# A hybrid attention layer on one core: c's parts through a view, the first weights ahead of x, one bias addition for tile 0

## The chip, the core and the metric

The kernel runs on one core of a Trainium2 chip. A core has five engines, each with its own instruction queue: TensorE (PE in the profile; PEld is its loading of stationary weights), VectorE (DVE), ScalarE (ACT), GpSimd (POOL) and SyncE (SP, which here only issues transfers). Sixteen DMA engines move data between device memory (HBM) and the on-chip buffer (SBUF). TensorE writes its results to a third memory, PSUM. The engines run side by side and wait for each other through semaphores.

The metric is the device time of one execution in microseconds (us), taken as the median of a few runs.

## What is computed

One decoder layer for 512 positions of width 1024. All its inputs are float32. The part that matters here is the start: the conditioning vector c (1024 numbers) is multiplied by a large matrix, and the first two of the six resulting vectors shift and scale x before the input projection.

```python
mod = c @ w_ada + b_ada
sh1, sc1, gt1, sh2, sc2, gt2 = [m[:, None, :] for m in jnp.split(mod, N_MOD, axis=-1)]

u = x * (1.0 + sc1) + sh1
proj = u @ w_in
...
y_fox = _merge_heads(_forgetting_attention(...))
y_sb = _merge_heads(_stick_breaking_attention(...))
merged = jax.nn.sigmoid(g_a) * (y_fox @ w_fox_proj) + jax.nn.sigmoid(g_b) * (y_sb @ w_sb_proj)
attn_out = merged @ w_o
x = _layer_norm(DEEPNORM_ALPHA * x + (1.0 + gt1) * attn_out, ln1_g, ln1_b)
u2 = x * (1.0 + sc2) + sh2
h = _causal_depthwise_conv(u2 @ w_up, conv_w, conv_b)
h_gate, h_val = jnp.split(h, 2, axis=-1)
ffn_out = (jax.nn.silu(h_gate) * h_val) @ w_down
x = _layer_norm(DEEPNORM_ALPHA * x + (1.0 + gt2) * ffn_out, ln2_g, ln2_b)
```

## The kernel before

**Precision.** [...] So that a product keeps the precision of float32, each operand is split into a high part h (rounded by ScalarE, a copy into the type fp32r) and a low part l (the remainder, one subtraction on VectorE, helper `lo_of`, line 94). A product is then three matmuls: high by high, low by high and high by low. In the names below `wh`, `wl` are the parts of a weight and `uh`, `ul` those of u.

**Tiling.** The width of 1024 is cut into KT = 8 tiles of 128 rows. The opening works through them one after the other, j = 0 to 7. For each tile it loads two pieces of the modulation matrix (`wa`, one for the shift and one for the scale), the rows of x (`xt`, 128x512) and the first weights of the input projection (`raw`, 128x904: 904 columns, the last 8 being those of the forget gate). VectorE multiplies `wa` by c and sums along the row (`mod_sum`, line 231), which gives one shift and one scale per row (`modc`). From x it makes u and its two parts, and TensorE adds the tile's products to eight accumulators in PSUM (`grp`, line 349, 23 matmuls for a tile). Attention, the output projection and the gated MLP follow; they are not touched.

**How c reaches all partitions.** `mod_sum` needs the whole of c in every one of the 128 partitions. c arrives as 8 rows of 128 (`c8s`, line 102). VectorE splits it into three parts of type bf16 whose sum is c to full precision. They stand in rows 0 to 7, 32 to 39 and 64 to 71 of a tile `chl`: the first is a rounded copy (line 122, written as an addition of zeros), then comes the remainder in float32 (`c1`, line 123), the same remainder as bf16 (line 124), and what is left after that (line 125). Eight small matmuls (line 225) with a matrix `sel` of ones in rows k, 32+k and 64+k add the three parts and spread row k over all partitions, four into each of the two accumulators `grp[6]` and `grp[7]`. For tile 0 `mod_sum` reads c straight from these accumulators; later tiles read a copy of it in SBUF (`cbc`, line 325, made by ScalarE). For tile 0 the sums are taken in halves of 512 columns, so there are four: e is the half and q the vector (0 the shift, 1 the scale). After them two operations (line 277) add for each vector its two halves and the bias column `bcols`. ScalarE has added 1 to the columns of the scales beforehand (line 127).

**Warming matmuls.** TensorE runs matmuls without use (`heat`, line 220, on a tile of zeros): `WARM[0]` = 7 at the start, `WARM[1]` = 3 after the eight that spread c, and `WARM[2]` = 1 after each of the sums of tile 0 but the first (`paced` makes them wait for that sum).

**Loads.** SP issues the loads in an order written out by hand (`tc.manual_schedule` for that engine alone; for the other engines the framework's planner works out the order, within the edges that `issue_after` draws). For tile 0 (`first_load`, lines 247 to 249): the two `wa`, then `xw`, which is one packed array of x's 512 columns and the first 384 columns of the weights, then the other 520 columns of the weights into `raw`. Then come the loads of tile 1 (lines 251 to 257) and, two tiles ahead from there, the rest. c and the biases go out from ScalarE's queue (lines 102 and 104).

**Tile 0 behind the sums.** `first_split` makes the high part of the 384 columns (line 289); `first_mod` makes `uh` on VectorE (line 317), u itself on ScalarE (line 319), the high part of the other 520 columns (line 322), the copies of c (line 325), and on VectorE the low parts. In `first_mm` the matmuls of the first 384 columns stand ahead of those of columns 384 to 639. For the tiles after it (j > 0), ScalarE first makes the high part of all 904 columns (line 91, called from `first_split`), then `uh` (line 306) and u (line 311).

Of the kernel before, what the change touches and what calls it, by code (L numbers as in the profile page):

```python
# [8 lines left out]
F32 = mybir.dt.float32  # L9
F32R = mybir.dt.float32r  # L10
BF16 = mybir.dt.bfloat16
AF = mybir.ActivationFunctionType
ALU = mybir.AluOpType
# [3 lines left out]
P = 128  # L17
T = 512
D = 1024
KT = D // P  # L20
# [22 lines left out]
GS = 7  # L43
SS = 10
GTILES = (3, 5, 7, 8, 12, 16, 20, 24)
WARM = 7, 3, 1
CUT = 5
FILL = (15, 18, 18), (11, 11, 11)


@with_exitstack
def layer_kernel(ctx: ExitStack, tc: tile.TileContext, out, xT, x, c8, wa0, wa1, bcol, xw, w1, wct, wv, bf,
                 wp, wo, lncol, lnrow, wup, cwb, wdp):
    nc = tc.nc
    ctx.enter_context(tc.manual_schedule(engines={nc.sync.engine}))
    V, S, G, PE = nc.vector, nc.scalar, nc.gpsimd, nc.tensor
# [12 lines left out]
    early = st0.enter_context(tc.tile_pool(name="early", bufs=1))  # L69

    cnt, state = [0], {"load": 0, "proc": 0}
# [12 lines left out]
    def const(shape, dt, s):  # L84
        return cons.tile(shape, dt, name=s, tag=s)

    def fl(ap):
        return ap.bitcast(F32)
# [4 lines left out]
    def lo_of(o, i, hi):  # L93
        state["read"] = V.tensor_tensor(o, i, fl(hi), ALU.subtract)  # L94
        return state["read"]

    def preset(shape, dt, s):
        return pre.tile(shape, dt, name=s, tag=s)

    cbc = preset([P, D], F32, "cbc")  # L100
    c8s = early.tile([KT, P], F32, name="c8s", tag="c8s")
    S.dma_start(c8s, c8)
    bcols = const([P, 6, KT], F32, "bcols")
    bcd = S.dma_start(bcols, bcol)
    warm = early.tile([P, 512], BF16, name="warm", tag="warm")
# [1 line left out]

    ident = const([P, P], F32, "ident")
    ones = const([P, P], F32, "ones")
    chl, sel = early.tile([P, P], BF16, name="chl", tag="chl"), early.tile([P, KT], BF16, name="sel", tag="sel")  # L110
    c1 = early.tile([KT, P], F32, name="c1", tag="c1")
    G.memset(chl, 0.0)
    G.memset(ones, 1.0)
    sgt = const([P, 1], F32, "sgt")
    with tc.issue_after(bcd.ins):
# [2 lines left out]
    s3 = early.tile([P, KT], F32, name="s3", tag="s3")  # L118
    V.tensor_tensor(s3, ident[:, 0:KT], ident[:, 32:40], ALU.add)
    s = V.tensor_tensor(sel, s3, ident[:, 64:72], ALU.add)  # L120
    with tc.issue_after(s.ins):
        V.tensor_tensor(chl[0:KT], c8s, warm[0:KT, 0:P], ALU.add)
    V.tensor_tensor(c1, c8s, chl[0:KT], ALU.subtract)
    V.tensor_tensor(chl[32:40], c8s, chl[0:KT], ALU.subtract)
    state["chl"] = V.tensor_tensor(chl[64:72], c1, chl[32:40], ALU.subtract)
    for q in (slice(1, 2), slice(3, 6)):
        S.activation(bcols[:, q, :], bcols[:, q, :], AF.Copy, bias=1.0)
    mska = preset([P, 512], F32, "mska")
# [7 lines left out]
    modc = const([P, 4, KT], F32, "modc")  # L136
    modr = const([P, 6, KT, 2], F32, "modr")
# [81 lines left out]
    def heat(n):  # L219
        return [PE.matmul(grp[5], warm[:, 0:P], warm, start=True, stop=True) for _ in range(n)]  # L220

    heat(WARM[0])
    for k in range(KT):
        o = grp[6 + k // 4][:, k % 4 * P : (k % 4 + 1) * P]
        m = PE.matmul(o, sel[:, k : k + 1].broadcast_to([P, P]), chl, start=True, stop=True)
    with tc.issue_after(m.ins):
        heat(WARM[1])

# [7 lines left out]
        b, o = bcols[:, w, col : col + 1], modc[:, w, col : col + 1]  # L236
        return V.tensor_tensor(o, modr[:, w, col, 0:1], b, ALU.add)

    xw0 = early.tile([P, 896], F32, name="xw0", tag="xw0")

    def first_load(j):
        wa = [early.tile([P, D], F32, name=nm("wa"), tag="wa", bufs=5) for _ in range(2)]
        r = stg.tile([P, 1024], F32, name=nm("raw"), tag="raw", bufs=LOADS)
        xt = z(F32, "xt")
        if j == 0:
            for e in range(2):
                nc.sync.dma_start(wa[e], wa0[j, e])
            nc.sync.dma_start(xw0, xw)
            nc.sync.dma_start(r[:, 384:W1C], w1[j][:, 384:W1C])
        else:  # L250
            nc.sync.dma_start(wa[0], wa0[j, 0])
            if j == 1:
                nc.sync.dma_start(wa[1], wa0[j, 1])
            nc.sync.dma_start(r[:, 0:W1C], w1[j])
            if j > 1:
                nc.sync.dma_start(wa[1], wa0[j, 1])
            nc.sync.dma_start(xt, xT[j * P : (j + 1) * P, :])
            if j == 6:
                nc.sync.dma_start(bfs, bf)
        pend[j] = [wa, xt, r]  # L260

    def first_acc(j):
        wa = pend[j][0]
        if j == 0:
            s = state["chl"]
            for e in range(2):
                for q in range(2):
                    c = slice(q * 512, (q + 1) * 512)
                    with tc.issue_after(s.ins):
                        s = mod_sum(q, j, wa[e], c, e, grp[6 + e])  # L270
                    if e or q:
                        for m in heat(WARM[2]):
                            paced(m, s)
            for q in range(2):
                raw = modr[:, q, j, :]
                with tc.issue_after(s.ins):
                    s = state["modc"] = V.scalar_tensor_tensor(modc[:, q, j : j + 1], raw[:, 0:1], raw[:, 1:2], bcols[:, q, j : j + 1], ALU.add, ALU.add)
        else:
            mod_col(0, j, wa[0])
            state["modc"] = mod_col(1, j, wa[1])  # L280

    def first_split(j):
        r = pend[j][2]
        h = stg.tile([P, 1024], F32R, name=nm("wh"), tag="wh", bufs=WBUFS)
        l = stg.tile([P, 1024], F32R, name=nm("wl"), tag="wl", bufs=WBUFS)
        if j:
            hi_of(h[:, 0:W1C], r[:, 0:W1C])
        else:
            state["h"] = S.activation(h[:, 0:384], xw0[:, 512:896], AF.Copy)
        pend[j][2:] = [h, l, r]  # L290

    def first_pad(j):
# [8 lines left out]
    def first_mod(j):  # L301
        wa, xt = pend[j][0:2]
        sh, sc = modc[:, 0, j : j + 1], modc[:, 1, j : j + 1]
        a, b = z(F32R, "uh"), z(F32R, "ul")
        if j:
            u = S.activation(a, xt, AF.Identity, bias=sh, scale=sc)
            h, l, r = pend[j][2:]
            with tc.issue_after(state["modc"].ins):
                state["after"] = lo_of(l[:, 0:W1C], r[:, 0:W1C], h[:, 0:W1C])
            with tc.issue_after(u.ins):  # L310
                u = state["u"] = S.activation(xt, xt, AF.Identity, bias=sh, scale=sc)
            with tc.issue_after(state["after"].ins):
                state["after"] = lo_of(b, xt, a)
        else:
            h, l, r = pend[j][2:]
            with tc.issue_after(state["modc"].ins):
                ts = V.tensor_scalar(a, xw0[:, 0:512], sc, sh, ALU.mult, ALU.add)
            with tc.issue_after(state["h"].ins):
                u = S.activation(xt, xw0[:, 0:512], AF.Identity, bias=sh, scale=sc)
            c = slice(384, W1C)  # L320
            with tc.issue_after(u.ins):
                u = S.activation(h[:, c], r[:, c], AF.Copy)
            for e in range(2):
                with tc.issue_after(u.ins):
                    u = state["u"] = S.activation(cbc[:, e * 512 : (e + 1) * 512], grp[6 + e], AF.Copy)
            with tc.issue_after(ts.ins):
                ts = lo_of(l[:, 0:384], xw0[:, 512:896], h[:, 0:384])
            with tc.issue_after(ts.ins):
                state["after"] = lo_of(b, xt, a)
        with tc.issue_after(u.ins), tc.issue_after(state["after"].ins):  # L330
            first_pad(j)
        uh.append(a)
        ul.append(b)
# [17 lines left out]
    for j in range(2):  # L351
        first_load(j)
# [391 lines left out]
    for p, nb in (6, 3), (7, 5):  # L744
        add_pair(p)
        for _ in range(nb):
            j = bj.pop(0)
# [255 lines left out]
    for n in range(2 * FT):  # L1003
        wui.append(add_item(wup[n], split_proc))
        if n in GTILES:
            k = GTILES.index(n)
            wai[(10, 28)[k // 4]] = add_item(wa1[(28, 24)[k // 4] + k % 4], ada_proc((28, 24)[k // 4] + k % 4))
        if n in (15, 19):
            p = (15, 19).index(n)
            add_item(wdp[p][:, 1024:1536], scale_proc(wgt[p]), 512)  # L1010
        if n in (23, 27):
            t = t13[(23, 27).index(n)][:, 0:512]
# [5 lines left out]
        if n in (28, 31, 32, 35):  # L1018
            k = (28, 31, 32, 35).index(n)
# [116 lines left out]
    for n in range(2 * FT):  # L1136
        if n < NSPLIT:
            h, l = items[wui[n]][4]
            ps = bks[n]
            up_mm(ps, h, l, slice(256, 512))  # L1140
        else:
            ps = bank()
            h, l = weights(wui[n], min(LOADS - 1, wui[min(n + 2, 2 * FT - 1)] - wui[n]))
# [20 lines left out]
        t = z(F32, "cv")  # L1164
# [26 lines left out]
    r = x1  # L1191
# [126 lines left out]
def _pack(inputs):  # L1318
    import numpy as np

    a = {k: np.ascontiguousarray(v) for k, v in inputs.items()}
    c = np.ascontiguousarray
    w_in, w_ada = a["w_in"], a["w_ada"]
    r = {}
    r["xT"] = c(a["x"][0].T)
    r["x"] = a["x"][0]
    r["c8"] = c(a["c"][0].reshape(KT, P))
    wt = c(w_ada.T).reshape(6, KT, P, D)
    wa0 = wt[0:2].transpose(1, 0, 2, 3).copy()
    wa0[0] = wa0[0].reshape(2, P, 2, D // 2).transpose(2, 1, 0, 3).reshape(2, P, D)  # L1330
# [4 lines left out]
    def col(kind, n):  # L1335
        if kind in ("sb", "fox"):
# [4 lines left out]
    first = [w_in[:, s : s + P] for s in [col("q", 0), col("k", 0)] + [col("sb", j) for j in range(NG)]]  # L1341
    cols = np.concatenate(first + [w_in[:, 1536:1544]], axis=1)
    r["w1"] = c(cols.reshape(KT, P, W1C))
    r["xw"] = c(np.concatenate([r["xT"][0:P], cols[0:P, 0:384]], axis=1))
    wv = np.stack([w_in[:, 1024:1536], w_in[:, 2568:3080]])
    r["wv"] = c(wv.reshape(2, 4, 2, P, 512).transpose(0, 1, 3, 2, 4).reshape(2, 4, P, D))
    starts = [col(*t) for t in TILES]
# [14 lines left out]
    return r  # L1362


_NAMES = ["xT", "x", "c8", "wa0", "wa1", "bcol", "xw", "w1", "wct", "wv", "bf", "wp", "wo", "lncol", "lnrow",
          "wup", "cwb", "wdp"]


# [17 lines left out]
```

## Time and profile before

| | us |
|---|---|
| median of 3 runs | 737.15 |
| lowest and highest of them | 737.0 and 739.07 |
| the profiled execution, its own time | 736.59 |
| its span, from first to last instruction | 734.8 |

| engine | busy us | share of the span |
|---|---|---|
| TensorE, matmuls | 724.6 | 99% |
| TensorE, weight loads (beside them) | 605.4 | 82% |
| VectorE | 600.3 | 82% |
| ScalarE | 389.9 | 53% |
| GpSimd | 84.8 | 12% |

How to read the lines that follow. In the timeline each line has a start and a duration in us, the engine, the line of the kernel, the operation, what it writes and reads, the shape, a count where several are merged, and in brackets the idle time before it with what ended it. A queue (SPq, ACTq) is the engine's own instruction queue, where transfers are issued; the transfer itself lands later. In the chain that ended last, the profile goes back from the last instruction, at each step to what released it or to the one before it on its engine. The lists of waits give engine, line and who was waited for. Matmuls are pipelined and their ends are modelled, so that the spacing of their starts says more than their durations.

### The profile page before, as it was taken

How to read it: one execution, taken by the hardware profiler on the slowest of the kernel's cores; microseconds unless marked ns; L12 is line 12 of the kernel's file. 1: busy time of each engine (PE TensorE's matmuls, PEld its weight loads, DVE VectorE, ACT ScalarE, POOL GpSimd, SP SyncE). 2: the span in 40 equal slices, each digit the busy share in tenths (PEclk: the TensorE clock that was granted, in tenths of full speed). 3: DMA queues.
4: the chain of work that ended last, by engine and by line, in shares of the span. 5: the costliest groups of instructions: out<-in, count | busy, mean ns of one | idle time of the engine just before them, and what ended most of it. 6: DMA issues, size and time to landing. Idle time of an engine off the chain costs nothing.

```text
span 734.8 us, 9844 instructions
## 1 busy us (share of the span) xinstructions
PE 724.6 (99%) x3443; PEld 605.4 (82%) x3443; DVE 600.3 (82%) x1051; ACT 389.9 (53%) x681; POOL 84.8 (12%) x139
## 2 busy tenths in 40 slices
PE   8999999999999999999999999999999999999995
PEld 5888888888888888888889888888888888888884
DVE  7878889778898886883697989988887778679995
ACT  4576466686885755432065543454453444446550
POOL 1026224353010000000000001000011001000010
PEclk9999999999999999999999999999999999999998
DMA  9944534423332241632075678587699767656733
GB/s 355 405 163 141 199 116 163 181 85 103 131 116 82 92 157 73 207 143 86 1 258 136 214 235 245 176 249 228 186 347 265 214 222 213 206 173 213 243 76 84
DMA packets 45059, 131.96 MB, mean 180 GB/s; under 512 B 6121, under 2 KB 6513, under 8 KB 45009
## 3 DMA queue, kind: packets, MB, share of 16 engines
q1 hardware_dynamic: 37744, 112.61, 44.1%
q0 software_dynamic: 4224, 10.30, 7.2%
q10 hardware_dynamic: 3040, 8.42, 3.1%
q8 instruction: 27, 0.44, 0.2%
q14 instruction: 24, 0.19, 0.1%
HBM read 118.39 MB, written 12.85 MB: 179 GB/s over the span
## 4 chain that ended last, share of the span: by engine, by line
PE 98%; DVE 1%; DMA 1%; issue 0%; ACTq 0%; DVEq 0%
PE ps L145 19%; PE ps L147 19%; PE ps L146 19%; PE ps L349 6%; PE ps L1113 5%; PE ps L1114 5%; PE ps L1115 5%; PE ps L587 3%; PE ps L569 2%; PE ps L495 2%; PE ps L497 2%; PE ps L496 2%; PE ps L910 2%; PE ps L911 2%; PE ps L912 2%; PE ps L521 1%
## 5 line engine op out<-in xcount | busy, mean ns | idle before, releaser
L208 ACT ACTIVATE wh<-raw 128x1024 fp32r<-128x1024 f32 (+1 forms) x105 | 109.1, 1041 | 106.3 <-PE ps L146 37.1
L94 DVE TENSOR_TENSOR wl<-raw,wh 128x1024 fp32r<-128x1024 f32 (+3 forms) x113 | 136.4, 1209 | 32.0 <-ACT wh L208 31.7
L145 PE MATMUL ps<-u2h,wh 128*128 128x512 f32 (+1 forms) x376 | 141.4, 376 | 0.0
L146 PE MATMUL ps<-u2l,wh 128*128 128x512 f32 (+1 forms) x376 | 141.2, 376 | 0.0
L147 PE MATMUL ps<-u2h,wl 128*128 128x512 f32 (+1 forms) x376 | 141.2, 375 | 0.0
L145 PEld LDWEIGHTS ps<-u2h,wh 128*128 128x128 f32 x376 | 70.8, 188 | 12.8
L147 PEld LDWEIGHTS ps<-u2h,wl 128*128 128x128 f32 x376 | 70.8, 188 | 12.7
L146 PEld LDWEIGHTS ps<-u2l,wh 128*128 128x128 f32 x376 | 70.8, 188 | 12.7
L145 PE MATMUL ps<-uh,wh 128*128 128x512 f32 x200 | 79.5, 398 | 0.0
L147 PE MATMUL ps<-uh,wl 128*128 128x512 f32 x200 | 78.3, 391 | 0.0
L146 PE MATMUL ps<-ul,wh 128*128 128x512 f32 x200 | 77.9, 390 | 0.0
L1166 ACT ACTIVATE cv<-ps,cw 128x512 f32<-128x512 f32 x44 | 33.9, 771 | 39.9 <-PE ps L147 28.5
L1167 DVE SCALAR_TENSOR_TENSOR cv<-ps,cw,cv 128x511 f32<-128x511 f32 x44 | 32.8, 745 | 21.4 <-ACT cv L1166 21.4
L147 PEld LDWEIGHTS ps<-uh,wl 128*128 128x128 f32 x200 | 37.5, 188 | 8.6 <-DVE wl L94 0.3
L146 PEld LDWEIGHTS ps<-ul,wh 128*128 128x128 f32 x200 | 37.6, 188 | 7.4
L145 PEld LDWEIGHTS ps<-uh,wh 128*128 128x128 f32 x200 | 37.6, 188 | 7.4
L231 DVE SCALAR_TENSOR_TENSOR raw<-raw,cbc 128x1024 f32<-128x1024 f32 x32 | 39.5, 1238 | 0.0
L549 POOL TENSOR_TENSOR pt<-pt,om 128x127 f32<-128x127 f32 (+3 forms) x32 | 39.1, 1231 | 1.1 <-DVE om L548 1.0
L174 POOL DMA_DIRECT2D raw<-in_wdp x10 | 9.2, 915 | 245.2 <-DMA raw<-in_wdp 210.4
L1174 ACT ACTIVATE cv<-cv 128x512 f32<-128x512 f32 x22 | 13.9, 631 | 36.9 <-DVE cv L1168 36.8
L1168 DVE SCALAR_TENSOR_TENSOR cv<-ps,cw,cv 128x510 f32<-128x510 f32 x44 | 32.7, 743 | 0.4
L548 DVE TENSOR_TENSOR_SCAN om<-om,dg 128x127 f32<-128x127 f32 (+3 forms) x32 | 27.3, 913 | 3.6 <-ACT om L543 3.6
(239 smaller groups left out, 1554.7 us busy)
## 6 DMA issues: line engine op xcount, KB each, us to landing
raw<-in_wup SPq DMA_DIRECT2D x44, 512.0 KB, 4.9
raw<-in_wa SPq DMA_DIRECT2D x32, 512.0 KB, 3.6
raw<-in_wct SPq DMA_DIRECT2D x25, 512.0 KB, 4.5
raw<-in_wdp SPq DMA_DIRECT2D x20, 512.0 KB, 5.2
wa<-in_wa SPq DMA_DIRECT2D x16, 512.0 KB, 7.9
raw<-in_wdp SPq DMA_DIRECT2D x22, 256.0 KB, 4.8
raw<-t SPq DMA_DIRECT2D x22, 256.0 KB, 4.4
raw<-in_wdp POOLq DMA_DIRECT2D x10, 512.0 KB, 8.2
```

Source lines behind the costliest of these rows:

```text
L94: state["read"] = V.tensor_tensor(o, i, fl(hi), ALU.subtract)
L145: PE.matmul(ps, wh, ah, start=first, stop=False)
L146: PE.matmul(ps, wh, al, start=False, stop=False)
L147: return PE.matmul(ps, wl, ah, start=False, stop=last)
L208: state["hi"] = S.activation(h[:, 0:cols], r[:, 0:cols], AF.Copy)
L231: state["read"] = V.scalar_tensor_tensor(wt[:, c], wt[:, c], 1.0, cbc[:, c] if by is None else by, ALU.mult, ALU.mult, accum_out=o)
L349: PE.matmul(grp[g], w, u, start=j == 0 and n == 0, stop=j == KT - 1 and n == (1 if g == 7 else 2))
L549: G.tensor_tensor(pt[b][:, s : e - 1], pt[b][:, s : e - 1], om[:, s + 1 : e], ALU.mult)
L1113: PE.matmul(ps, ah, bh, start=first, stop=False, skip_group_check=onto)
L1114: PE.matmul(ps, ah, bl, start=False, stop=False, skip_group_check=onto)
L1115: return PE.matmul(ps, al, bh, start=False, stop=last, skip_group_check=onto)
L1166: S.activation(t, ps, AF.Identity, bias=cw[:, n, 3:4], scale=cw[:, n, 2:3])
```

## The change

Three edits in the opening, and what goes with them.

*c's parts.* c is loaded as 32 rows (8 of them c, the others zeros, put there by the host) into rows 0 to 31 of a float32 tile `crow`. `ctop` is a view of that tile: the upper 16 bits of each float32 word read as a bf16 number, so every second bf16 element. The first part of c is the view of its rows, with no operation. Two subtractions then make the other parts: rows 32 to 63 are rows 0 to 31 less their view, rows 64 to 95 are rows 32 to 63 less theirs. The matmuls that spread c read all 128 rows of the view; rows 96 to 127 are zeroed by GpSimd. `c1`, `chl` and the four operations on lines 122 to 125 go.

*First weights.* The packed array `xw` goes. SP loads the first 384 columns of tile 0's weights into their place in `raw`, then x's rows into a tile `x0`, then the other 520 columns of the weights: three transfers where there were two.

*Biases of tile 0.* After the first sum of the second halves (e = 1, q = 0), one addition on two columns puts the sums of the first halves onto the biases of both vectors. After the last sum, one addition on two columns makes `modc`. The two operations of line 277 go.

With them, `WARM[0]` goes from 7 to 5, and the last sum is followed by two warming matmuls instead of one.

```diff
-WARM = 7, 3, 1
+WARM = 5, 3, 1
...
-    c8s = early.tile([KT, P], F32, name="c8s", tag="c8s")
-    S.dma_start(c8s, c8)
+    crow = early.tile([P, P], F32, name="crow", tag="crow")
+    S.dma_start(crow[0:32, :], c8)
...
-    chl, sel = early.tile([P, P], BF16, name="chl", tag="chl"), early.tile([P, KT], BF16, name="sel", tag="sel")
-    c1 = early.tile([KT, P], F32, name="c1", tag="c1")
-    G.memset(chl, 0.0)
+    sel = early.tile([P, KT], BF16, name="sel", tag="sel")
+    G.memset(crow[96:128, :], 0.0)
...
-    with tc.issue_after(s.ins):
-        V.tensor_tensor(chl[0:KT], c8s, warm[0:KT, 0:P], ALU.add)
-    V.tensor_tensor(c1, c8s, chl[0:KT], ALU.subtract)
-    V.tensor_tensor(chl[32:40], c8s, chl[0:KT], ALU.subtract)
-    state["chl"] = V.tensor_tensor(chl[64:72], c1, chl[32:40], ALU.subtract)
+    ctop = crow.bitcast(BF16).rearrange("p (c t) -> p c t", t=2)[:, :, 1]
+    for k in (0, 32):
+        with tc.issue_after(s.ins):
+            s = state["chl"] = V.tensor_tensor(crow[k + 32 : k + 64, :], crow[k : k + 32, :], ctop[k : k + 32, :], ALU.subtract)
...
-        m = PE.matmul(o, sel[:, k : k + 1].broadcast_to([P, P]), chl, start=True, stop=True)
+        m = PE.matmul(o, sel[:, k : k + 1].broadcast_to([P, P]), ctop, start=True, stop=True)
...
-            nc.sync.dma_start(xw0, xw)
+            nc.sync.dma_start(r[:, 0:384], w1[j][:, 0:384])
+            nc.sync.dma_start(x0, xT[j * P : (j + 1) * P, :])
             nc.sync.dma_start(r[:, 384:W1C], w1[j][:, 384:W1C])
...
-                        for m in heat(WARM[2]):
+                        for m in heat(WARM[2] + e * q):
                             paced(m, s)
-            for q in range(2):
-                raw = modr[:, q, j, :]
-                with tc.issue_after(s.ins):
-                    s = state["modc"] = V.scalar_tensor_tensor(modc[:, q, j : j + 1], raw[:, 0:1], raw[:, 1:2], bcols[:, q, j : j + 1], ALU.add, ALU.add)
+                    if e and not q:
+                        with tc.issue_after(s.ins):
+                            s = V.tensor_tensor(bcols[:, 0:2, j], bcols[:, 0:2, j], modr[:, 0:2, j, 0], ALU.add)
+            with tc.issue_after(s.ins):
+                state["modc"] = V.tensor_tensor(modc[:, 0:2, j], modr[:, 0:2, j, 1], bcols[:, 0:2, j], ALU.add)
...
-            state["h"] = S.activation(h[:, 0:384], xw0[:, 512:896], AF.Copy)
+            state["h"] = S.activation(h[:, 0:384], r[:, 0:384], AF.Copy)
...
-                ts = V.tensor_scalar(a, xw0[:, 0:512], sc, sh, ALU.mult, ALU.add)
+                ts = V.tensor_scalar(a, x0, sc, sh, ALU.mult, ALU.add)
...
-                u = S.activation(xt, xw0[:, 0:512], AF.Identity, bias=sh, scale=sc)
+                u = S.activation(xt, x0, AF.Identity, bias=sh, scale=sc)
...
-                ts = lo_of(l[:, 0:384], xw0[:, 512:896], h[:, 0:384])
+                ts = lo_of(l[:, 0:384], r[:, 0:384], h[:, 0:384])
...
-    r["c8"] = c(a["c"][0].reshape(KT, P))
+    r["c8"] = np.zeros((32, P), np.float32)
+    r["c8"][0:KT] = a["c"][0].reshape(KT, P)
```

More of the change, by code (lines that the diff above doesn't have):

```diff
@@ L51, in layer_kernel @@
 @with_exitstack
-def layer_kernel(ctx: ExitStack, tc: tile.TileContext, out, xT, x, c8, wa0, wa1, bcol, xw, w1, wct, wv, bf,
+def layer_kernel(ctx: ExitStack, tc: tile.TileContext, out, xT, x, c8, wa0, wa1, bcol, w1, wct, wv, bf,
                  wp, wo, lncol, lnrow, wup, cwb, wdp):
@@ L237, in mod_col @@
         return V.tensor_tensor(o, modr[:, w, col, 0:1], b, ALU.add)
-    xw0 = early.tile([P, 896], F32, name="xw0", tag="xw0")
+    x0 = early.tile([P, 512], F32, name="x0", tag="x0")
     def first_load(j):
@@ L1343, in _pack @@
     r["w1"] = c(cols.reshape(KT, P, W1C))
-    r["xw"] = c(np.concatenate([r["xT"][0:P], cols[0:P, 0:384]], axis=1))
     wv = np.stack([w_in[:, 1024:1536], w_in[:, 2568:3080]])
@@ L1362, in _pack @@
     return r
-_NAMES = ["xT", "x", "c8", "wa0", "wa1", "bcol", "xw", "w1", "wct", "wv", "bf", "wp", "wo", "lncol", "lnrow",
+_NAMES = ["xT", "x", "c8", "wa0", "wa1", "bcol", "w1", "wct", "wv", "bf", "wp", "wo", "lncol", "lnrow",
           "wup", "cwb", "wdp"]
```

## The prediction

> **What bounds the kernel now.** I read the page first, then who waited for whom on TensorE, then the chain that ended last in order of time, then the timeline of the first 19 us. The page's head, its busy shares and the shares of the chain:
>
> ```profile
> span 734.8 us, 9844 instructions
> ...
> PE 724.6 (99%) x3443; PEld 605.4 (82%) x3443; DVE 600.3 (82%) x1051; ACT 389.9 (53%) x681; POOL 84.8 (12%) x139
> ...
> PE 98%; DVE 1%; DMA 1%; issue 0%; ACTq 0%; DVEq 0%
> ```
>
> The waits of TensorE over the whole span (engine, line, what it waited for: us in total, times, longest):
>
> ```profile
> PE ps L220 <- DVE warm L106: 1.2, 1, 1.2
> PE ps L349 <- DVE uh L317: 0.6, 1, 0.6
> ```
>
> These are all its waits: one before the first warming matmul, one before the first real one (L349). After that TensorE waits for nothing until its work ends. So the change is worth what it takes from the start of L349, less any wait that it opens behind it. The chain in order of time:
>
> ```profile
> 1.38 4.31 DMA bcols<-in_bcol
> ...
> 6.05 1.30 DVE wa L231 x5
> ...
> 7.72 0.56 DVE uh L317
> 8.28 0.14 issue
> 8.41 42.28 PE ps L349 x184
> ```
>
> L349 starts at 8.41, behind uh (L317, 7.72), behind four sums of VectorE (L231). The bcols transfer, landed at 1.38 + 4.31 = 5.69, is put into the chain only because VectorE's queue passed a wait then; the timeline shows the sums back to back across it:
>
> ```profile
> 0.74 0.60 ACTq L102 DMA_DIRECT2D c8s<-in_c  x1
> 0.75 0.85 SPq L247 DMA_DIRECT2D wa<-in_wa  x2
> 1.65 0.44 SPq L248 DMA_DIRECT2D xw<-in_xw  x1
> ...
> 2.72 0.28 DVE L122 TENSOR_TENSOR chl<-c8s,warm 8x128 bf16<-8x128 f32 x1 [0.24 <-DMA c8s<-in_c]
> ...
> 3.04 0.28 DVE L123 TENSOR_TENSOR c<-c8s,chl 8x128 f32<-8x128 f32 x1
> ...
> 3.64 0.28 DVE L125 TENSOR_TENSOR chl<-c,chl 8x128 bf16<-8x128 f32 x1
> ...
> 3.98 0.97 PEld L225 LDWEIGHTS <-sel 128*128 128x128 bf16 x8 [0.52 <-DVE chl L125]
> 4.16 1.06 PE L225 MATMUL ps<-chl,sel 128*128 128x128 bf16 x8
> 4.20 0.36 SPq L257 DMA_DIRECT2D xt<-in_xT  x1
> 4.83 0.69 DVE L231 SCALAR_TENSOR_TENSOR wa<-wa,ps 128x512 f32<-128x512 f32 x1 [0.90 <-PE ps L225]
> ...
> 5.71 0.32 ACT L127 ACTIVATE bcols<-bcols 128x8 f32<-128x8 f32 x2 [2.43 <-DMA bcols<-in_bcol]
> ...
> 6.66 0.68 DVE L231 SCALAR_TENSOR_TENSOR wa<-wa,ps 128x512 f32<-128x512 f32 x1
> ...
> 7.27 0.42 DVE L277 SCALAR_TENSOR_TENSOR modc<-modr,bcols 128x1 f32<-128x1 f32 x2
> 7.27 0.52 ACT L289 ACTIVATE wh<-xw 128x384 fp32r<-128x384 f32 x1 [1.24 <-DMA xw<-in_xw]
> ...
> 7.72 0.55 DVE L317 TENSOR_SCALAR uh<-xw,modc 128x512 fp32r<-128x512 f32 x1
> ```
>
> The reader should see a serial path (c lands, four operations, eight matmuls, four sums, two bias additions, uh) and, beside it, a transfer almost as late: ScalarE got xw at 7.27, only 0.45 before uh began.
>
> **The change part by part.** Landing times come from the view of DMA issues in narrow windows (KB each, us from issue to landing):
>
> ```profile
> wa<-in_wa SPq DMA_DIRECT2D x1, 512.0 KB, 3.4
> ...
> wa<-in_wa SPq DMA_DIRECT2D x1, 512.0 KB, 4.2
> xw<-in_xw SPq DMA_DIRECT2D x1, 448.0 KB, 5.6
> ...
> raw<-in_w SPq DMA_DIRECT2D x1, 260.0 KB, 5.8
> ...
> xt<-in_xT SPq DMA_DIRECT2D x1, 256.0 KB, 8.1
> ```
>
> *c's parts.* L122 to L125 start (3.64 - 2.72) / 3 = 0.31 apart; two exact remainders replace the four. If c lands as before, they start at 2.72 and 3.03, and the weight load of L225 follows the last by 3.98 - 3.64 = 0.34, at 3.37: 0.61 earlier. Seven warming matmuls would now stand in the way (they end where L225 starts, at 4.16); five at their pace of about 0.43 end at 3.34, so the shorter WARM costs and brings nothing itself. The first sum comes 0.67 behind the first L225, as now: 4.22. Its weights landed at 0.75 + 3.4 = 4.15. The second pair, issued about 1.19, landed at 5.39, and the third sum wants it at 5.44. Both just fit; a slip of 0.1 in either transfer shows one for one.
>
> Two costs here are unknown. TensorE reads the parts as bf16 words 4 bytes apart: from nothing (L349 streams 4-byte words without such a loss, below) to double the L225 pitch of about 0.11, 0.43 over the four matmuls that the first sum needs. I take nothing. And c comes as 32 rows, where 8 landed by 2.72: bounds are no delay and a landing like that of bcols at 5.69; the nearest row is c's own, so I take 0.05.
>
> *Biases.* The one addition moves in behind the third sum, at 6.05. It needs ScalarE's L127, done at 5.71 + 0.32 = 6.03, so the wait it adds costs nothing, but everything behind it on VectorE (fourth sum, modc, uh) would slip by whatever bcols is late. It pushes the fourth sum by 0.13 to 0.22 (an L277 is 0.42 / 2 = 0.21; the nearest row, a plain addition such as L237 below, is two in 0.28). Behind the last sum the path hardly shortens: now the second L277 starts only when the accumulator is out, and the first hides in that time, so one addition in place of two saves at most 0.06. Net a loss of about 0.1. VectorE is ready for uh at 7.72 - 0.61 + 0.05 + 0.1 = 7.26 (7.15 to 7.35).
>
> *First weights ahead of x.* The same bytes in two transfers instead of one: h no longer waits for x, but h was not last. x0 now ends where xw ended, 1.65 + 5.6 = 7.25, plus about 0.1 for 128 more packets and c's larger rows. SP has one issue of 0.44 more, and each later load is issued that much later; as they land 5.8 to 8.1 us after issue, from a stream that is full (below), this hides, and would cost up to 0.44 if the stream ran dry. So uh starts at 7.35, bound by x and VectorE alike, and L349 at 7.35 + (8.41 - 7.72) = 8.04: **0.37 earlier**.
>
> *What is late next.* The second weight tile. Timeline and windows (PE busy, PEld, DVE, ACT, POOL; clock; DMA share; GB/s):
>
> ```profile
> 11.62 0.96 ACT L91 ACTIVATE wh<-raw 128x904 fp32r<-128x904 f32 x1 [1.50 <-DMA raw<-in_w]
> ...
> 12.36 0.28 DVE L237 TENSOR_TENSOR modc<-modr,bcols 128x1 f32<-128x1 f32 x2
> ...
> 12.67 0.82 ACT L306 ACTIVATE uh<-xt,modc 128x512 fp32r<-128x512 f32 x1
> ...
> 13.74 1.30 PE L349 MATMUL ps<-uh,wh 128*128 128x512 f32 x5
> ...
> 14.89 1.30 PE L349 MATMUL ps<-uh,wl 128*128 128x512 f32 x5
> ```
> ```profile
> 17.66 0.82 ACT L306 ACTIVATE uh<-xt,modc 128x512 fp32r<-128x512 f32 x1 [2.00 <-DVE modc L237]
> ```
> ```profile
> 8.41:13.74 5.33, 5.33 (x23) 4.40 (x24) 5.26 (x11) 3.71 (x8) 0.00 (x0) 1.00 1.03 415
> 13.74:18.98 5.24, 5.24 (x25) 4.32 (x23) 4.27 (x9) 2.95 (x5) 0.00 (x0) 1.00 1.03 408
> ```
>
> Tile 0 takes TensorE 5.33, so it would be free at 8.04 + 5.33 = 13.37. Tile 1 needs uh(1) from L306, which stands on ScalarE behind L91, and L91 waited 1.50 for its weights until 11.62. The DMA share is 1.03: this stream cannot come earlier, and its bytes are the same. VectorE's modc(1) moves from 12.64 to 12.27, but x's next rows land at 4.20 + 8.1 = 12.3 and L91 ends at 11.62 + 0.96 = 12.58, with up to 0.1 more for the extra packets. L306 so starts near 12.60 instead of 12.67, and TensorE gets its result at 12.60 + 0.82 + 0.14 = 13.56. It waits 0.19, and **0.18 of the 0.37 is left** (0.1 to 0.25). Tile 2 has room: 17.66 + 0.82 + 0.14 = 18.62 against 13.56 + 5.24 = 18.80. From there nothing was late before and the order is the same, so the shift should reach the end. Sum: 736.59 for the profiled run less 0.18 is 736.4; the median of the runs shown lies 0.56 above that run, at 737.15, so I forecast **737.0**.
>
> **The rivals.** *The loads of tile 1 do not hold it.* If the stream happens to run 0.2 sooner, the 0.37 passes whole, or up to 0.55 with x earlier too: 736.6 to 736.8. Against it: L91's 1.50 of waiting.
>
> *c lands late (slower).* Its 32 rows are issued at 0.74 beside the first weights at 0.75, and rows queued behind those land with them: bcols, issued 0.64 later, took 4.31. The path breaks even when c lands 0.45 late, at about 3.2. If c lands with the first weights at 4.15, the weight load of L225 comes at 4.15 + 0.31 + 0.34 = 4.80, 0.82 later than now, and the bias addition adds 0.1: 738.1; like bcols, at 5.69, 739.6. For it: the small transfer has four times the rows. Against: it is issued first, and 8 rows were in by 2.72.
> [...]
>
> *TensorE stays at half pace longer.* The clock column says 1.00 throughout the opening, so the pace is read from the matmuls:
>
> ```profile
> 1.20 3.17 PE L220 MATMUL ps<-warm 128*128 128x512 bf16 x7 [1.20 <-DVE warm L106]
> ```
> ```profile
> 7.41 0.39 PE L220 MATMUL ps<-warm 128*128 128x512 bf16 x1
> ```
>
> Seven in 3.17 is 0.45 or a little less each; at tile 1 five take 14.89 - 13.74, 0.23 each, and the last warming matmul (7.41, 0.39) already has the duration of those (1.30 - 4 x 0.23 = 0.38). The step came after some 6 us of nearly gapless work. The change leaves gaps of 0.2 to 0.4 around L225 and the bias addition. If the step fell at 10.6, six real matmuls would cost 0.20 more each: 1.2, less the 0.19 of waiting that this covers and the 0.18 gained, near 738.0; a whole tile at half pace, 23 x 0.20 = 4.6, gives 741.6. Decisive is whether the step comes before 8.04.
> [...]
>
> *Another order.* Only SP's order is written out by hand; a planner works out the other engines', and a changed opening may swap neighbours later. TensorE has no wait there now, so it can mostly lose; nothing in the trace prices it; I allow 1 either way.
>
> **How the numbers follow.** Forecast 0.58; tile 1 not binding 0.14; c late 0.11; half pace longer 0.09; another order 0.08. A measurement of this kernel can tell about 0.3%, 2.2 us, from no change. Only the far ends of the last three cross it: slower 0.05, faster 0.02, within 0.93. The range takes the second case at its low end, less the scatter between runs (0.15 below the median), and c late or half pace at their first prices with the scatter above: 736.1 to 738.6.
>
> **What would show it.** L225's weight load at 3.4; the first sum at 4.2; no gap on VectorE before the bias addition; x0 at 7.25 to 7.4; L349 at 8.0; then a new wait of about 0.2 on TensorE at the start of tile 1, for L306. Wrong would be: c landing past 3.2, L349's first matmuls 0.43 apart, or any TensorE wait past 19 us. If tile 1 starts with no wait, the step on the stream was wrong.

## The result and the profile after

| | before | after |
|---|---|---|
| median of 22 runs | 736.72 us (736.26 to 739.13) | 736.08 us (735.75 to 736.97) |
| profiled execution | 736.59 us, span 734.8 | 736.11 us, span 734.3 |

The ratio is 0.9988, with a 95% interval of 0.9983 to 0.9994: a small gain, 0.64 us by the medians. (The ratio is not that of the two medians, which would be 0.9991.) It lies within 0.3%, as forecast, but the time is 0.02 below the low end of the range, and the gain is more than three times the 0.18 that was worked out. Of the 0.92 between 737.0 and 736.08, the base has 0.43 (the three runs of before had a median of 737.15, the 22 have 736.72) and the size of the gain 0.46 (0.64 less 0.18); the rest is rounding.

The head of the page after says the same as before: TensorE is busy throughout.

```profile
span 734.3 us, 9843 instructions
...
PE 724.5 (99%) x3442; PEld 605.2 (82%) x3442; DVE 600.0 (82%) x1049; ACT 390.1 (53%) x681; POOL 84.9 (12%) x139
```

The timeline of the opening after (start, length, engine, line, and in brackets the idle time ahead with what ended it):

```profile
3.60 0.60 DVE L123 TENSOR_TENSOR crow<-crow 32x128 f32<-32x128 f32 x2 [0.99 <-DMA crow<-in_c]
...
4.25 1.03 PE L223 MATMUL ps<-crow,sel 128*128 128x128 bf16 x8 [0.74 <-DVE crow L123]
...
4.90 0.69 DVE L229 SCALAR_TENSOR_TENSOR wa<-wa,ps 128x512 f32<-128x512 f32 x1 [0.70 <-PE ps L223]
...
6.72 0.16 DVE L275 TENSOR_TENSOR bcols<-bcols,modr 128x2 f32<-128x2 f32 x1
...
6.80 0.68 DVE L229 SCALAR_TENSOR_TENSOR wa<-wa,ps 128x512 f32<-128x512 f32 x1
...
7.40 0.08 DVE L229 DVE_READ_ACCUMULATOR wa<-wa,ps 128x1 f32 x1
...
7.52 0.16 DVE L277 TENSOR_TENSOR modc<-modr,bcols 128x2 f32<-128x2 f32 x1
...
7.72 0.55 DVE L317 TENSOR_SCALAR uh<-x,modc 128x512 fp32r<-128x512 f32 x1
...
8.41 1.05 PE L349 MATMUL ps<-uh,wh 128*128 128x512 f32 x3
...
9.30 0.84 PE L349 MATMUL ps<-uh,wl 128*128 128x512 f32 x3
...
13.85 1.32 PE L349 MATMUL ps<-uh,wh 128*128 128x512 f32 x5
```

uh begins at 7.72 and L349 at 8.41, to a hundredth where they stood before. VectorE takes c at 3.60 instead of 2.72, so the two operations saved are spent on waiting. The view of DMA issues (us to landing last) has c's 32 rows, issued at 0.74, and x, issued at 2.13:

```profile
crow<-in_c ACTq DMA_DIRECT2D x1, 16.0 KB, 2.8
...
x<-in_xT SPq DMA_DIRECT2D x1, 256.0 KB, 4.9
```

Tile 1 begins 0.11 later than before (13.85 against 13.74). None of the gain in this execution comes from the opening, nor from TensorE's long middle. The chain in order of time at the end shows the first operation that depends on the last matmul (L1313) and the last normalizing one (L1214), of before:

```profile
726.51 0.43 DVE xn L1313
...
730.74 0.40 DVE xn L1214
```

and of after:

```profile
726.57 0.43 DVE xn L1313
...
730.80 0.40 DVE xn L1214
```

Until there the changed kernel is 0.06 *behind*. From the start of L1313 to the end of the span it was 734.8 - 726.51 = 8.3, and is 734.3 - 726.57 = 7.7 (8.30 and 7.78 before the rounding of the spans, a gain of 0.52); VectorE's part of it is 4.23 in both. What is left is the output. The timeline of SP's queue from 728.5 on (three output transfers in one row: start, and from the first issue to the end of the last) and the view of DMA issues and queues from 729 on, of before:

```profile
730.37 1.60 SPq L1215 DMA_DIRECT2D out<-xn  x3
```
```profile
q14 instruction: 1, 0.01, 0.3%
...
out<-xn SPq DMA_DIRECT2D x1, 256.0 KB, 2.4
out<-xn SPq DMA_DIRECT2D x2, 128.0 KB, 2.2
```

and of after, where the first of these views is again the timeline and the second the DMA issues:

```profile
730.44 1.30 SPq L1215 DMA_DIRECT2D out<-xn  x3
```
```profile
q1 hardware_dynamic: 432, 0.52, 22.4%
...
out<-xn SPq DMA_DIRECT2D x1, 256.0 KB, 2.1
out<-xn SPq DMA_DIRECT2D x2, 128.0 KB, 2.1
```

Three issues take 1.60 before and 1.30 after, and their landing is 0.1 to 0.3 shorter. In the same stretch before has a row that after lacks: one packet of 0.01 MB on q14, the queue whose kind the profile calls instruction. The expectations below take it for a fetch of instructions; what it brings, and for which engine, no view shows. It is not gone after, it has moved ahead, to the window from 727.5 to 729.5, between SP's issues at 726.31 and 730.44, in which SP waits 3.7 for VectorE (queues of that window, after):

```profile
q14 instruction: 1, 0.01, 2.2%
```

Narrow windows show where the 0.30 lies. SP's first two issues one by one, in before:

```profile
730.37 0.33 SPq L1215 DMA_DIRECT2D out<-xn  x1
...
731.14 0.33 SPq L1215 DMA_DIRECT2D out<-xn  x1
```

and the second of them in after, whose first stands at 730.44:

```profile
730.88 0.37 SPq L1215 DMA_DIRECT2D out<-xn  x1
```

From the end of the first to the start of the second it is 0.44 in before and 0.11 in after. The packet itself is not there. In before the last of the three issues ends at 730.37 + 1.60 = 731.97; the DMA queues from 729 to 731.98 have no q14, and those from 732 to 734 have it:

```profile
q14 instruction: 1, 0.01, 1.0%
```

So SP had issued all three transfers before that packet moved.

The change gives SP one more transfer to issue (the first weights apart from x). This suggested that the length of SP's instruction stream, not the opening, had made the gain. It had to be tested.

### The profile page after: what moved, and what is told of

Read it like the earlier page. It is cut to its first block, busy times and chain, and to the rows that moved or that the text cites. A ratio compares the mean times of both kernels' runs of the same rounds, so it can differ in the third digit from the quotient of the medians.

```text
span 734.3 us, 9843 instructions
## 1 busy us (share of the span) xinstructions
PE 724.5 (99%) x3442; PEld 605.2 (82%) x3442; DVE 600.0 (82%) x1049; ACT 390.1 (53%) x681; POOL 84.9 (12%) x139
## 4 chain that ended last, share of the span: by engine, by line
PE 98%; DVE 1%; DVEq 0%; issue 0%
PE ps L143 19%; PE ps L145 19%; PE ps L144 19%; PE ps L349 6%; PE ps L1113 5%; PE ps L1115 5%; PE ps L1114 5%; PE ps L587 3%; PE ps L569 2%; PE ps L495 2%; PE ps L497 2%; PE ps L496 2%; PE ps L912 2%; PE ps L910 2%; PE ps L911 2%; PE ps L521 1%
## 5 line engine op out<-in xcount | busy, mean ns | idle before, releaser
L94 DVE TENSOR_TENSOR wl<-raw,wh 128x1024 fp32r<-128x1024 f32 (+2 forms) x114 | 137.4, 1207 | 29.9 <-ACT wh L206 29.6
```

## The experiments

Four theories stand in the expectations below. **A**: c's 32 rows always land late beside the first weights. **B**: c's landing varies from execution to execution, and the profile after happened to show a late one. **C**: the gain lies behind the last matmul and belongs to one more transfer in SP's queue. **D**: the gain lies in the opening. Each kernel was timed in 11 or 10 runs beside 33 of the kernel before on the same chip. All results in one table; the last three columns are from one profile each (c is taken up where VectorE's first operation on it starts):

| kernel | SP transfers against before | ratio (95%) | medians apart, us | c taken up | uh | L1313 to the end |
|---|---|---|---|---|---|---|
| sp_minus1_before | -1 | 0.9999 (0.9990 to 1.0008) | +0.14 | 2.70 | 7.36 | 8.51 |
| b0 (before itself) | 0 | 1.0000 (0.9991 to 1.0009) | +0.07 | 2.56 | 7.72 | 8.29 |
| only_c | 0 | 1.0005 (0.9996 to 1.0013) | -0.06 | 3.50 | 7.70 | 8.28 |
| only_bias | 0 | 0.9999 (0.9990 to 1.0008) | -0.25 | 2.41 | 7.37 | 8.30 |
| load_neutral | 0 | 0.9997 (0.9988 to 1.0006) | -0.29 | 2.48 | 7.40 | 8.25 |
| sp_minus1 | 0 | 0.9997 (0.9988 to 1.0006) | -0.36 | 3.51 | 7.64 | 8.31 |
| a0 (the change) | +1 | 0.9990 (0.9981 to 0.9999) | -0.60 | 3.47 | 7.60 | 7.78 |
| change_again | +1 | 0.9993 (0.9984 to 1.0002) | -0.56 | 3.50 | 7.62 | 7.77 |
| no_c | +1 | 0.9991 (0.9982 to 1.0000) | -0.69 | 2.40 | 7.37 | 7.78 |
| only_load | +1 | 0.9988 (0.9979 to 0.9997) | -0.82 | 2.43 | 7.72 | 7.78 |
| sp_plus1 | +1 | 0.9994 (0.9985 to 1.0003) | -0.69 | 2.40 | 8.00 | 7.78 |
| sp_plus1_again | +1 | 0.9996 (0.9987 to 1.0004) | -0.59 | 2.75 | 7.67 | 7.78 |
| fast_c | +1 | 0.9986 (0.9977 to 0.9995) | -0.81 | 2.55 | 7.21 | 7.79 |
| fast_c_again | +1 | 0.9990 (0.9981 to 0.9999) | -0.78 | 2.60 | 7.38 | 7.79 |
| c_first | +2 | 1.0013 (1.0004 to 1.0022) | +1.31 | 2.63 | 7.88 | 7.78 |
| sp_plus3 | +3 | 0.9997 (0.9988 to 1.0006) | -0.17 | 2.40 | 7.90 | 7.66 |

**The two kernels again.** b0 is before, a0 and change_again are the change, unedited.

> The kernel before, against itself: what a comparison shows where nothing differs, and a second profile of it. Both theories: ratio 1.000 within 0.0006. Profile: c taken up by VectorE near 2.7 us, L349 from 8.4, the last matmul ending near 726.5. What lies behind the last matmul was 8.3 us in the first profile of before and 7.8 in that of after: if that is a property of each kernel it is 8.3 again, if chance it is anywhere between.

> The changed kernel again. Theory A (c's 32 rows always stand behind the first weights): VectorE takes c up near 3.6 again, L349 starts near 8.4 and the last matmul ends near 726.5, so that any gain lies behind the last matmul (7.8). Theory B (c's landing differs from execution to execution, and the first profile caught a late one): c is taken up anywhere from 2.7 to 3.6, and where it is early L349 starts 0.3 to 0.6 sooner. Ratio near 0.999 by both.

> The whole change, a third time: c taken up near 3.5, end 7.8, ratio 0.9990 to 0.9993 (the end, and little from the opening).

The gain came back twice (-0.60, -0.56), and before against itself gives nothing. c was late in both new profiles too, and in all five profiles in which its 32 rows are issued from ScalarE (3.47 to 3.60, against 2.40 to 2.75 wherever its 8 rows are; at 2.40 to 2.48 VectorE did not wait for them): B falls, A stands. The profiled run of a0 was 737.09 all the same: TensorE lost 0.8 in it far behind the opening, at one wait that the profiles of before and after don't show:

```profile
PE ps L143 <- DVE cv L1168: 0.8, 1, 0.8
```

That is the scatter against which one profile must be read.

**One part of the change at a time.** Each is before with the hunks of one part (the WARM counts that belong to it too); no_c has those of only_load and only_bias.

```diff
only_c:    + S.dma_start(crow[0:32, :], c8)
           + ... crow[k + 32 : k + 64, :], crow[k : k + 32, :], ctop[k : k + 32, :], ALU.subtract)
only_load: + nc.sync.dma_start(r[:, 0:384], w1[j][:, 0:384])
           + nc.sync.dma_start(x0, xT[j * P : (j + 1) * P, :])
only_bias: + s = V.tensor_tensor(bcols[:, 0:2, j], bcols[:, 0:2, j], modr[:, 0:2, j, 0], ALU.add)
```

> c's parts alone (with 5 warming matmuls), loads and biases as before. Theory A: c near 3.6, the two operations saved (0.6) are spent on the later landing (0.8), uh near 7.9, ratio 1.000 to 1.0005. Theory B: c earlier in most executions, uh bound by xw at about 7.3, ratio 0.9993 to 0.9997.

> The split loads alone (three transfers where there were two). Theory C (the gain lies behind the last matmul and belongs to the one transfer more on SP's queue): the end behind the last matmul is 7.8 instead of 8.3, L349 starts near 8.4 as before, ratio 0.9993. Rival D (the gain is in the opening, because the first weights come ahead of x, or in the bias addition): the end stays 8.3.

> The one bias addition alone (with the second warming matmul behind the last sum). From the traces: 2.83 instead of 2.89 from the first sum to uh, hidden or not by xw's landing; L349 0.06 earlier at most; SP's queue as before, so the end is 8.3 and the ratio 0.9997 to 1.0000. If the bias addition had a share of its own in the gain: 0.9993 or less.

> The change without c's part: loads in three and the one bias addition, c as before. Theory A: if c's part gives nothing, this has the whole gain of the change, ratio near 0.9988. Theory B: the bias addition in the middle costs 0.1 and the split loads bring nothing, so ratio 1.0000 to 1.0003; uh near 7.8.

c's part alone is worth nothing. The view of DMA issues and the timeline of only_c show why; its landing is no accident of the other parts:

```profile
crow<-in_c ACTq DMA_DIRECT2D x1, 16.0 KB, 2.7
```
```profile
3.50 0.60 DVE L123 TENSOR_TENSOR crow<-crow 32x128 f32<-32x128 f32 x2 [0.90 <-DMA crow<-in_c]
```

Of the three parts only the load has an interval without 1, although its uh begins at 7.72, as before. only_bias begins L349 at 8.06, 0.35 earlier, and still its interval holds 1. Most of that is not its addition: in its execution TensorE had reached full pace before L225, whose eight matmuls took 0.61 instead of 1.06, so that the sums began earlier. Timeline of only_bias:

```profile
4.12 0.61 PE L225 MATMUL ps<-chl,sel 128*128 128x128 bf16 x8
```

no_c owes its early uh to the same (its L225 took 0.61, from 4.11); load_neutral has uh nearly as early, at 7.40. Where an edit and such a step fall together, one profile of the opening proves nothing about the edit.

**SP's transfers without the change, and the change without SP's transfer.** sp_plus1 (repeated as sp_plus1_again) is before, with bf loaded a second time into a tile that nobody reads (32 bytes). sp_minus1 is the whole change with one transfer handed from SP to ScalarE; load_neutral is only_load with the same edit.

```diff
sp_plus1:   nc.sync.dma_start(bfs, bf)
          + nc.sync.dma_start(bfs2, bf)
sp_minus1, load_neutral:
          - nc.sync.dma_start(bfs, bf)
          + S.dma_start(bfs, bf)
```

> The kernel before, with one transfer of 32 bytes more on SP's queue (the forget bias loaded a second time into a spare tile, at tile 6, some 28 us in); nothing of the change. Theory C: the end behind the last matmul is 7.8, the opening as before (L349 at 8.4), ratio 0.9993. Rival D: end 8.3, ratio 1.000.

> The kernel before with one transfer of 32 bytes more on SP's queue, again: end 7.8, ratio 0.9993 (0.52 of 737). xw's landing as it falls, 6.9 to 7.9.

> The whole change, with one transfer taken off SP's queue (the forget bias is issued from ScalarE instead, the number of SP's transfers is that of before). Theory C: the end behind the last matmul is back at 8.3 and the gain is gone, ratio 1.000. Rival D: end 7.8, ratio 0.999.

> The split loads alone, with SP's number of transfers as before (the forget bias issued from ScalarE): end behind the last matmul 8.3. If the split lets x land sooner than xw did: x's arrival at 7.0 to 7.1, uh never late for it, and a ratio of 0.9995 to 0.9998 (xw held uh up by 0.2 to 0.3 in some of the profiles, not in others). If all of the gain of the split loads was SP's count: 1.000.

sp_plus1 does useless work and nothing of the change, and its medians moved like the change's: -0.69 and -0.59. SP's timeline and the DMA queues from 729 on in sp_plus1 have the form of after, three issues in 1.30 and no packet of q14:

```profile
730.59 1.30 SPq L1217 DMA_DIRECT2D out<-xn  x3
```
```profile
q1 hardware_dynamic: 432, 0.52, 22.6%
```

sp_minus1, the whole change in SP's old count, has the form of before:

```profile
730.44 1.60 SPq L1215 DMA_DIRECT2D out<-xn  x3
```
```profile
q14 instruction: 1, 0.01, 0.3%
...
out<-xn SPq DMA_DIRECT2D x1, 256.0 KB, 2.4
out<-xn SPq DMA_DIRECT2D x2, 128.0 KB, 2.2
```

C is borne out. Single intervals of sp_plus1 reach 1.0003 and 1.0004, so no single one shows it; the order of all does. With SP's count unchanged the medians are 0.36 below to 0.07 above before, in five kernels; with one transfer more, 0.56 to 0.82 below, in eight comparisons of five kernels, whatever else they change; the two groups don't overlap.

**Two further counts.** sp_minus1_before takes one transfer from SP in before (bf again); sp_plus3 adds three useless ones.

```diff
sp_minus1_before: - nc.sync.dma_start(bfs, bf)
                  + S.dma_start(bfs, bf)
sp_plus3:         + nc.sync.dma_start(bfs2, bf)   (three such tiles)
```

> The kernel before with one transfer fewer on SP's queue (the forget bias issued from ScalarE); nothing of the change. If the end is long because a fetch of instructions falls between SP's last output transfers, and each instruction more or less moves that place by one: with one fewer it falls before the second output transfer, still behind the first, so the end stays near 8.3, ratio 1.000. If any other number of transfers than before shortens the end: 7.8, ratio 0.9993.

> The kernel before with three more transfers of 32 bytes on SP's queue at tile 6. By the fetch theory its place is now in SP's idle time ahead of the last output transfers: end 7.8, the fetch early, ratio 0.9993. If only the parity or an exact number counts: 8.3.

The end is 8.51 with one transfer fewer and 7.66 with three more. In sp_plus3 the time did not follow (-0.17), so a short end alone does not decide the time: its TensorE is late, for its profile has L1313's counterpart at 735.3 - 7.66 = 727.6, against 726.5. Its xw landed 6.1 after the issue (5.6 before), which made uh 0.18 later, and one more wait cost 0.3:

```profile
PE ps L1116 <- DVE cv L1171: 0.3, 1, 0.3
```

Another 0.3 goes at 54.88, where L523 starts 0.42 behind the matmul ahead of it (0.11 in before). No run tells whether the three transfers cause this.

**c without its delay.** c_first issues c's 32 rows from SP, ahead of the first weights. fast_c keeps the other two parts and the two exact remainders, but loads c as 8 rows.

```diff
c_first: - S.dma_start(crow[0:32, :], c8)
         + nc.sync.dma_start(crow[0:32, :], c8)
fast_c:  + S.activation(crow[0:KT], c8s, AF.Copy)
         + V.tensor_tensor(crow[32:40], c8s, c8top, ALU.subtract)
         + V.tensor_tensor(crow[64:72], crow[32:40], ctop[32:40], ALU.subtract)
```

> The change with c's 32 rows issued from SP's queue, ahead of the first weights on the same queue, instead of from ScalarE's beside them. If the 32 rows come late because they stand behind rows of the first weights: VectorE takes c up at 2.7 or before, the sums start near 4.3 to 4.7 (the first weights are now issued some 0.4 later), L349 near 8.0. If 32 rows are slow by themselves: c near 3.5 again, L349 at 8.3 or later. SP has two transfers more than before: end behind the last matmul 7.8.

> The change with c in 8 rows again: c lands at 2.7, VectorE makes the two exact remainders in the view's way, ScalarE copies the first part meanwhile; loads, biases and 5 warming matmuls as in the change. Theory A (c's 32 rows land 0.8 late): the sums start near 4.2, L349 near 7.8 to 8.0, against 8.06 without c's part. Step on tile 1 of the prediction (L306 cannot come before 12.5): tile 1 then starts at 13.4 with a wait of 0.1 to 0.3, and the ratio is that without c's part, 0.9988 to 0.9991. If tile 1 does not hold it: 0.9985 or less.

> The change with c in 8 rows and two operations on VectorE, again: c at 2.6, L349 at 7.9 or sooner, tile 1 held near 13.5 by L306. If tile 1 holds it, 0.1 to 0.2 less time than the change: ratio 0.9987 to 0.9990. If it is worth its whole 0.5 at L349: 0.9984 or less.

In c_first the 32 rows land 1.7 after their issue, against 2.7 to 2.8 in after, a0, change_again and only_c, and are taken up at 2.63: it is not their number alone that makes them late. (They are issued ahead of the first weights and not beside them, and from SP's queue; no run parts the two.) The kernel is slower nonetheless (1.0013), and its timeline shows where:

```profile
4.82 0.69 DVE L229 SCALAR_TENSOR_TENSOR wa<-wa,ps 128x512 f32<-128x512 f32 x1 [1.59 <-DMA wa<-in_wa]
...
7.67 0.61 PE L218 MATMUL ps<-warm 128*128 128x512 bf16 x2 [0.29 <-DVE wa L229]
8.57 1.62 PE L349 MATMUL ps<-uh,wh 128*128 128x512 f32 x3 [0.30 <-DVE uh L317]
...
12.01 0.85 PE L349 MATMUL ps<-ul,wh 128*128 128x512 f32 x3
...
15.44 0.86 PE L349 MATMUL ps<-uh,wh 128*128 128x512 f32 x3
```

The first weights are now last, so VectorE stood still for 1.59, and the warming matmuls that are paced by its sums came with gaps of 0.77, 0.41 and 0.29. TensorE had been at full pace: the two warming matmuls at 7.67 take 0.61 together, with starts some 0.22 apart. Then it fell back to half pace for seven matmuls of tile 0 (which start 0.45 apart, from 8.57 to 11.27; 0.23 in before). The windows have it in the granted clock (behind the busy times of the engines; then DMA share and GB/s):

```profile
5.05:8.45 3.40, 1.74 (x6) 0.31 (x4) 3.19 (x12) 1.11 (x2) 0.00 (x0) 1.00 0.96 357
8.46:11.86 3.40, 3.29 (x8) 2.64 (x9) 3.38 (x7) 1.81 (x5) 0.00 (x0) 0.50 1.02 409
11.88:15.30 3.42, 3.42 (x17) 2.80 (x16) 2.64 (x7) 2.69 (x5) 0.00 (x0) 1.00 1.04 422
```

Tile 0 takes 15.44 - 8.57 = 6.87 instead of 5.33. With L349 0.16 later and the end 0.52 shorter that makes 1.54 + 0.16 - 0.52 = 1.2, against +1.31 by the medians. (Its one profile lost another 0.7 further on: L1313 stands at 736.7 - 7.78 = 728.9, 2.4 later than in before.)

fast_c has the opening that the prediction meant, uh at 7.21. Its timeline:

```profile
7.21 0.55 DVE L320 TENSOR_SCALAR uh<-x,modc 128x512 fp32r<-128x512 f32 x1
...
7.91 0.93 PE L352 MATMUL ps<-uh,wh 128*128 128x512 f32 x3 [0.27 <-DVE uh L320]
...
11.81 0.96 ACT L91 ACTIVATE wh<-raw 128x904 fp32r<-128x904 f32 x1 [2.01 <-DMA raw<-in_w]
...
13.01 0.39 PE L352 MATMUL ps<-ul,fpad 128*128 128x512 f32 x1
...
13.54 1.43 PE L352 MATMUL ps<-uh,wh 128*128 128x512 f32 x5
```

Its first real matmul is 0.50 earlier, but tile 1 is only 13.74 - 13.54 = 0.20 earlier: TensorE's last matmul of tile 0 starts at 13.01 and at its pace of 0.23 makes room at 13.24, 0.30 before tile 1 begins, and ScalarE's L91 waits 2.01 for tile 1's weights. The first five matmuls of tile 1 then take 1.43 instead of 1.30, so that behind them 0.07 of the 0.50 is left. Its medians are among the lowest (-0.81, -0.78; change_again, on the same chip as fast_c_again, has -0.56), but the intervals overlap: it is not shown to beat the change.

## Where the prediction was wrong, and where right

That the time fell, as forecast, is luck: the 0.37 that was to be won at L349 did not come (8.41 before and after), and the 0.52 that was won lies where the working did not look. The low end of the range, 736.1, does not follow from its own terms either: 736.6 less 0.15 is 736.45.

**What bounds the kernel** failed in one clause. It is right that TensorE binds from L349 to its last matmul. "The change is worth what it takes from the start of L349" and "the shift should reach the end" left out what lies behind that last matmul: 8.3 us, no part of which TensorE hides.

**First weights ahead of x** is the step that failed. "SP has one issue of 0.44 more, and each later load is issued that much later" priced the transfer as a delay of loads, at nothing with a bound of 0.44 *lost*. It did hide there. Its effect was at the other end of SP's stream: with one transfer more the packet of q14 moved from behind the issues of the last three output transfers (732 to 734 in before) into SP's wait ahead of them (727.5 to 729.5 in after), and the pause of 0.44 between SP's first two issues became 0.11. The issues took 0.30 less, and the rest of the 0.52 lies behind them, where the transfers land. By itself (sp_plus1) one transfer more moved the medians by -0.59 to -0.69, which is the change's -0.56 to -0.64; without it the change has -0.36 with an interval that holds 1. That the count sets the end is shown by counts from -1 to +3 (8.51 to 7.66). Why SP pauses is open. That the packet of q14 is the reason is the author's inference from the two moving together; no run moved it by other means. SP cannot have waited for what the packet brings before it issued the rest, as in before the packet moves only after 732 and the third issue ends at 731.97. x0 landed at about 7.0 (4.9 from its issue at 2.13), not at 7.35; it did not hold uh up. The 0.1 that the sum took for 128 more packets and c's larger rows was an estimate that no run shows.

**c's parts.** For c's landing, "so I take 0.05" was the wrong end of its bounds: VectorE took c up 0.75 to 0.88 later than in before. This, and not the loads, is why L349 came no earlier. The rival "c lands late" came true, but its price was wrong too. The path from c to the first matmul of L225 shrank not by 0.61 but by (4.16 - 2.72) - (4.25 - 3.60) = 0.79. The 0.61 is right up to the weight load; the 0.18 from there to the matmul (3.98 to 4.16 in before, both at 4.25 in after) goes too, as the warming matmuls no longer stand in it. (In no_c, which has all seven of them, c was taken up at 2.40, and L225 still began at 4.11.) So the path breaks even at 2.72 + 0.79 = 3.51, not at about 3.2, and 3.47 to 3.60 costs about nothing: only_c is 1.0005, uh 7.70. A wrong landing and a wrong break-even cancelled. Both landings taken for that rival, 4.15 and 5.69, were too late: in after c landed at 0.74 + 2.8 = 3.54, ahead of the first weights at 0.74 + 3.5 = 4.24.

**The view read by TensorE** (bf16 words 4 bytes apart) cost nothing, as taken: eight matmuls in 1.03, where before has 1.06.

**Biases** had the wrong sign, small. From the first sum to uh it was 7.72 - 4.83 = 2.89 and is 7.72 - 4.90 = 2.82. The addition in the middle pushes the fourth sum by 0.08 (6.72 to 6.80), not 0.13 to 0.22.

**Tile 1** could not be seen in the change, whose L349 came no earlier. In fast_c, which has the early L349, the step held: 0.50 went in and 0.20 came out, behind the weights of tile 1 (and 0.07 behind its first five matmuls). The forecast had 0.37 in and 0.18 out.

**Half pace** as a rival was rightly named. In after it shows in a trace: from the first L349 to the fourth it is 8.41 to 9.30, 0.89, where before has 8.41 to 9.18, 0.77; the 0.12 is what tile 1 is late by. In c_first it came in another way than the rival had it: the step to full pace was not late, the pace was lost again ahead of the first real matmul.

Whether a tenth or two of the gain comes from the opening stays open. load_neutral, sp_minus1 and only_bias have medians of -0.25 to -0.36 with intervals that hold 1. One way in which the loads could give it: VectorE waited for xw ahead of uh in two of the eight profiles of kernels that load it (0.32 in sp_plus1, 0.22 in sp_plus3), and for x0 in none of the other ten. How often that happens over many executions was not counted.

## What to carry to other kernels

Follow an edit's instructions on every queue to the end of the program, SP's too: here one transfer more cost nothing where it was added, and the stretch behind the last matmul was 7.78 us instead of 8.30, with the opening as late as before. Compare the stretch behind the last matmul on its own before giving a gain to the edit that was meant to make it, and run a control that adds a useless instruction in the same queue. Here c as 32 rows (16 KB) beside the first weights was there some 0.8 later than as 8 rows (taken up at 3.60 against 2.72), which undid the operations saved; work out the break-even from the whole path up to the consumer, waits included.

## What the runs showed of the hardware

The end behind the last matmul takes 8.51, 8.30, 7.78, 7.78 and 7.66 us with -1, 0, +1, +2 and +3 transfers in SP's queue, to within 0.05 in every profile of the same count (one profile each for -1, +2 and +3), although VectorE's operations there take 4.23 in each of before and after.

The step of TensorE to full pace (from 0.45 to 0.23 between the starts of matmuls of 512 columns) does not keep its time in nearly equal openings. It came before L225 at 4.1 in only_bias, at about 7.2 in before and about 8.7 in after, 2.9 to 7.5 after the first warming matmul, which began at 1.2 in each. It can also be lost again: in c_first TensorE was at full pace from 5.05 to 8.45 (six matmuls in 1.74 of these 3.40, granted 1.00), then granted 0.50 from 8.46 to 11.86, then 1.00. no_c kept the pace through gaps of 0.53, 0.22, 0.29 and 0.27, where c_first had 0.77, 0.41, 0.29 and 0.30; whether the gaps take the pace away, and which of them, no run here shows. The clock column says 1.00 also ahead of the first step, where the matmuls are at half pace, and shows only the later loss.
